# Applying the RMSNorm of the first token pair at the evictions, and moving weight fold and memory keys behind the first tiles

## The chip, the cores and the metric

One core of a Trainium2 chip runs the whole program. The metric is the device time of one execution in microseconds; three runs are shown, with their median.

## The reference

One layer of a streaming encoder on `x` (2048 tokens x 1024), f32:

```python
hn = rms_norm(x, norm_g)
proj = hn @ pool_w_in                       # 1024 -> u (768) | mq (256) | gate (1024)
u, mq, gate = split(proj)
# four groups of 192 columns: causal window means (2, 4, 8, 16) minus u, times w_group, times pool_scale
tok = multi_scale_pool(u, pool_w_group, pool_scale)
mem_k, mem_v = split(rms_norm(mem, mem_norm_g) @ w_mem_kv)   # 256 memory rows, 4 heads of 64
mem_o = softmax(mq @ mem_k.T / 8) @ mem_v
h = x + (concat(tok, mem_o) * silu(gate)) @ w_out
out = rms_norm(h, final_norm_g)
```

`rms_norm(x, g)` is `x * rsqrt(mean(x*x) + 1e-6) * g`, so a token's factor is one number that multiplies its whole projection.

## The kernel before, in words

Tokens are worked on transposed (channels on partitions) in four blocks of 512, two blocks making a pair. Every f32 product is three f32r products: each operand is split into a rounded high part and the rest (`_split`, L42 to L46), and `_mm3` (L49 to L53) adds high x high, high x low and low x high. A tile of weights is 128 output columns: 8 slices of 128 channels, 24 matmuls of 512 columns for each block. The first pair takes its tiles straight (`tile_in`, L425), 16 of them in the order of `TILES`: `q` are memory queries, `g` gates, `z` pooled columns. The second pair takes tiles two by two with seven products in place of eight (`group`, L388); its seven forms are prepared while the first pair runs (`stage_forms`, L238, four steps).

The pooled weights are folded first: `fold` (L280) multiplies the pooled part of `pool_w_in` by `w_group` in eight steps `k`, writes each into `w_z` in DRAM, and the `z` tiles load it from there. `wus` holds the eight loads `w_uT`, `wga` and `wgb` the group weights.

`first_block` (L211) makes a block ready: `squares` (L205) sums each row of `x` on ACT, `rstd_of` (L179) takes the power on POOL, `bcast_cols` (L191) broadcasts the four columns by matmuls with the identity, then for each of 8 slices DVE multiplies by gain and factor, ACT casts the high part and DVE subtracts the low one. So nothing of a block can be multiplied before its rows have been summed. `memory` (L324) makes `khi`, `klo` and `vhl` from `mem`, and `Attention` (L515) computes scores, softmax and mix in steps. `row_stats` (L230) sums the rows of the second pair and sends their factors through DRAM (`rows`).

`between()` is called after each half tile of a block; `Steps` (L691) counts these calls and runs the functions hooked to a number, and attention steps. That gives the order of the program; a scheduler then moves instructions within it by buffers and readiness, except loads that `load` (L115) keeps in program order. Each engine and each DMA queue (SP, ACT, POOL) runs its list in order. Tiles come from pools: `raw` has four buffers for loaded weights, `ch` four pairs for split weights, `ps_mm` four product banks, `sgp` two, `up` two.

The results leave a bank by a `take` function: queries are cast and subtracted straight from the bank (L446), gates go through Silu on ACT (L457), pooled columns are copied by ACT (L507). In the second pair `rest` is a tile to be added on DVE first (L104).

```python
fold()
xa = first_block(0)
xcol.append(load_columns(1, (8, 9)))
loaded = load_memory()
TILES = [("q", 0, (0,)), ("q", 1, (0,)), ("g", 5, (0, 1)), ("q", 0, (1,)), ("q", 1, (1,))]
hooks = {8: [lambda: memory(loaded)], 16: [stats]}
```

Of the kernel before, what the change touches and what calls it, by code (L numbers as in the profile page):

```python
# [56 lines left out]
def trunk(ctx, tc, x, xT, mem, memT, norm_g, mem_norm_g, w_mem, w_out, w_in, w_uT, w_g, p_scale, final_g,  # L57
# [53 lines left out]
    for _ in range(7):  # L111
        nc.tensor.matmul(idle, lhsT=zeros[:, :P], rhs=zeros, start=True, stop=True)
# [7 lines left out]
    wga = raw_tile((P, 4, GD))  # L120
    wgb = st.tile([P, 2, GD], F32, name="s")
    wus = [t[:, :6 * P].rearrange("p (g d) -> p g d", g=6) for t in long_tiles() + [zz((P, D)) for _ in range(4)]]
    for g in range(0, 4, 2):
        load(out=wga[:, g:g + 2], in_=w_g[g:g + 2, 0:128, :].rearrange("g c e -> c g e"))
        load(out=wus[0][:, g:2 + 2 * g], in_=w_uT[0, :, g:2 + 2 * g])
    for l in range(2):
        load(out=wgb[64 * l:64 * l + 64], in_=w_g[l::2, 128:192, :].rearrange("g c e -> c g e"))
    for k in range(1, KT):
        load(out=wus[k], in_=w_uT[k])
# [23 lines left out]
    xrow = [load_rows_of(0, (8, 9), load)]  # L153
    xcol = [load_columns(0, (12, 13))]
    ahead = [load_tile(w_in[j], load) for j in range(2)]
    xrow.append(load_rows_of(1, (10, 11), load))
# [29 lines left out]
    def rows_sq(src, t, acc):  # L186

        sp.dma_start(out=t, in_=src)
        nc.scalar.activation(out=t, in_=t, func=AF.Square, accum_out=acc)
# [21 lines left out]
    def first_block(a):  # L211

        rb = sgp.tile([P, BT], F32, name="sg")
        bcast_cols(squares(xrow[a]), QT, rb)
        hl = [(slot(2 * a + 4 * kh), slot(2 * a + 4 * kh + 1)) for kh in range(2)]
        for k in range(KT):
            v = xcol[a][k // KH][:, k % KH, :]
# [12 lines left out]
    def row_stats(s):  # L230

        rows = dram.tile([2, QT, P], F32, name="rows")
        for a in range(2):
            r = load_rows_of(2 * s + a, (10 + 2 * a, 11 + 2 * a), sp.dma_start)
            sp.dma_start(out=rows[a].rearrange("t p -> p t"), in_=squares(r))
        return rows
# [43 lines left out]
    def fold():  # L280

        tails = [[pl.tile([P, 2, GD], F32R, name=n) for _ in range(2)] for pl, n in ((att, "pr"), (up, "u"))]
# [6 lines left out]
        for k in range(KT):  # L289
            zs = wus[k].rearrange("p g d -> p (g d)")  # L290
            ut = ch.tile([P, 2, 2, P], F32R, name=("wh", "wl")[k % 2])
            nc.scalar.copy(ut[:, 0], wus[k][:, 4:6, :])
            nc.gpsimd.tensor_tensor(out=ut[:, 1], in0=wus[k][:, 4:6, :], in1=ut[:, 0].bitcast(F32), op=ALU.subtract)
            pss = [ps_mm.tile([P, 2, GD], F32, name="mm") for _ in range(2)]
            for a, ps in enumerate(pss):
                for l in range(2):
                    nc.tensor.matmul(ps[:, l, :], lhsT=wus[k][:, 2 * a + l, :], rhs=wga[:, 2 * a + l, :], start=l == 0,
                                     stop=False)
                _mm3(nc, ps, ut[:, 0, a, :], ut[:, 1, a, :], tails[0][a], tails[1][a], False, True)
# [3 lines left out]
            nc.scalar.dma_start(out=w_z[:, :, k, :].rearrange("j p f -> p j f"), in_=wus[k])  # L303
# [11 lines left out]
    def load_memory():  # L315
        mts = [long("mq").rearrange("p (k n) -> p k n", k=4) for _ in range(2)]
        wrs = [long(n) for n in ("pth", "ptl")]
        for c in range(2):
            load(out=mts[c], in_=memT[c])
        for c in range(2):  # L320
            load(out=wrs[c].rearrange("p (k n) -> p k n", k=2), in_=w_mem[c])
        return mts, wrs

    def memory(loaded):  # L324
        mh, ml = ([zz((P, 4, NMEM), F32R) for _ in range(2)] for _ in range(2))
        ssm = small.tile([P, 2], F32, name="ssm", bufs=1)
        mts, wrs = loaded
# [9 lines left out]
        for c in range(4):  # L337
            if c > 1:
                wrs.append(long("mq"))
                sp.dma_start(out=wrs[c].rearrange("p (k n) -> p k n", k=2), in_=w_mem[c])  # L340
            wr = wrs[c].rearrange("p (k n) -> p k n", k=2)
# [10 lines left out]
        for t in range(2):  # L352
            rows_sq(mem[t * P:(t + 1) * P, :], long(("pth", "ptl")[t]), ssm[:, t:t + 1])
        rm = rstd_of(ssm, 2)
        rmb = up.tile([P, NMEM], F32, name="u")
# [32 lines left out]
    def group(X, pair, take, between):  # L388
# [26 lines left out]
        take(0, 0, product(2, 1), None)  # L415
# [5 lines left out]
        take(1, 1, p7, u4)  # L421
        take(0, 1, product(3, 5), u2)
        take(1, 0, product(4, 7), u2)

    def tile_in(xs, wr, take, between):  # L425

        ps = {a: ps_mm.tile([P, BT], F32, name="mm") for a in xs}
        for kh in range(2):
            hi, lo = chunk(wr[:, kh * KH:(kh + 1) * KH], "act", (P, KH, P))
# [5 lines left out]
        for a in xs:  # L435
            take(0, a, ps[a], None)

    def take_query(s, p0):
        def take(i, a, ps, rest):
            p = p0 + i  # L440
            src = ps
            if rest is not None:
                src = sgp.tile([P, BT], F32, name="sg")
                add(nc.vector, src, ps, rest)
# [6 lines left out]
    def take_gate(s, j):  # L451
        def take(i, a, ps, rest):
# [8 lines left out]
    def take_pool(s, j0):  # L461
# [39 lines left out]
        def take(i, a, ps, rest):  # L501
# [6 lines left out]
            else:  # L508
                add(nc.vector, v, ps, rest)
# [176 lines left out]
    fold()  # L686
    xa = first_block(0)
    xcol.append(load_columns(1, (8, 9)))
    loaded = load_memory()
# [15 lines left out]
    def tile_of(s, kind, j, xs, between):  # L705
        if kind == "q":
            wr = ahead.pop(0) if ahead else load_tile(w_in[j])
            tile_in(xs, wr, take_query(s, j), between)
        elif kind == "g":
            tile_in(xs, load_tile(w_in[2 + j]), take_gate(s, j), between)  # L710
        else:
            tile_in(xs, load_tile(w_z[j]), take_pool(s, j), between)

    state = {}
    X1 = {}

    def stats():
        sp.dma_start(out=ci, in_=cinv)
        state["rows"] = row_stats(1)

    def stage(k):
        if not X1:
# [105 lines left out]
```

## Time and profile before

| | |
|---|---|
| three runs, us | 663.74, 663.86, 664.25 (median 663.86) |
| the profiled execution's own time, us | 666.16 |
| its span, first to last instruction, us | 664.4 |
| granted TensorE clock, mean | 0.955 |
| busy: PE, weight loads, DVE, ACT, POOL | 606.2, 505.6, 405.7, 332.2, 147.9 us |
| moved by DMA | 125.47 MB, mean 189 GB/s |

PE is TensorE's matmuls, PEld its weight loads, DVE VectorE, ACT ScalarE, POOL GpSimd; SPq, ACTq and POOLq are the queues that issue DMAs. Clock 1.00 is 2.4 GHz and half of it 1.2. In a row of the trace `mm<-x,wh` says what an instruction writes and reads, and an idle time in brackets names who ended it. Shares over the span are means over stretches with different limits.

### The profile page before, as it was taken

The numbers are of one execution on the slowest core, as the hardware profiler recorded it, in microseconds if no ns is written. First come the engines' busy times: TensorE is split into PE (matmuls) and PEld (weight loads), VectorE is DVE, ScalarE is ACT, GpSimd is POOL, SyncE is SP. The second block draws the span as 40 slices with busy tenths as digits, with TensorE's granted clock in tenths as the row PEclk, the third lists the DMA queues.
The fourth block names the chain that finished last, engine by engine and source line by source line (L and its number), as shares of the span: only waits on it lengthen the run. The fifth ranks groups of instructions, "written<-read, shape, count | busy, mean of one in ns | idle before, by whom it ended". The sixth has DMA issues, their size and how long they took to land.

```text
span 664.4 us, 8391 instructions
## 1 busy us (share of the span) xinstructions
PE 606.2 (91%) x2827; PEld 505.6 (76%) x2827; DVE 405.7 (61%) x677; ACT 332.2 (50%) x690; POOL 147.9 (22%) x157
## 2 busy tenths in 40 slices
PE   7649587799999999999999899998999999999993
PEld 6638476687787888888888688886788888888882
DVE  2055843748888446478578976799883436715126
ACT  3356741733766765474685398853652423214112
POOL 2101030115435113100006700163200001206016
PEclk7879689799998999999999899999999999999997
DMA  8999535675666541765441443337895136960006
GB/s 302 377 353 416 220 111 99 193 247 199 205 199 220 191 144 63 246 204 177 166 151 40 148 145 120 128 120 238 292 408 211 47 126 206 336 250 1 1 0 254
DMA packets 56123, 125.47 MB, mean 189 GB/s; under 512 B 7824, under 2 KB 17424, under 8 KB 56080
## 3 DMA queue, kind: packets, MB, share of 16 engines
q1 hardware_dynamic: 41056, 104.47, 46.5%
q10 hardware_dynamic: 13744, 16.27, 6.9%
q0 software_dynamic: 1280, 4.20, 1.7%
q8 instruction: 22, 0.36, 0.3%
q14 instruction: 21, 0.17, 0.1%
HBM read 87.68 MB, written 36.70 MB: 187 GB/s over the span
## 4 chain that ended last, share of the span: by engine, by line
PE 56%; DVE 15%; DMA 12%; ACT 8%; issue 5%; POOL 2%; SPq 1%; ACTq 0%; POOLq 0%; DVEq 0%
PE mm L52 13%; PE mm L51 13%; PE mm L53 13%; DVE wl L46 3%; DMA raw<-in_xT 2%; PE pt L52 2%; PE sc L53 2%; PE pt L53 2%; PE sc L52 2%; PE sc L51 2%; PE pt L51 2%; DMA w_z<-mq 2%; DVE zz L497 2%; DMA rows<-rstd 2%; DVE raw L101 1%
## 5 line engine op out<-in xcount | busy, mean ns | idle before, releaser
L51 PE MATMUL mm<-x,wh 128*128 128x512 f32 x480 | 192.2, 401 | 12.8 <-ACT wh L38 7.2
L52 PE MATMUL mm<-x,wh 128*128 128x512 f32 x480 | 190.6, 398 | 4.6 <-DVE x L46 4.6
L53 PE MATMUL mm<-x,wl 128*128 128x512 f32 x480 | 188.1, 396 | 0.0
L46 DVE TENSOR_TENSOR wl<-raw,wh 128x512 fp32r<-128x512 f32 x108 | 85.9, 802 | 87.5 <-ACT wh L38 87.5
L38 ACT CAST wh<-raw 128x512 fp32r<-128x512 f32 x108 | 66.2, 618 | 117.7 <-PE pt L53 80.0
L482 POOL TENSOR_TENSOR zz<-zz 128x527 f32<-128x527 f32 (+6 forms) x64 | 82.4, 1296 | 163.9 <-ACT zz L507 101.3
L51 PEld LDWEIGHTS mm<-x,wh 128*128 128x128 f32 x480 | 92.0, 192 | 32.3 <-ACT wh L38 7.9
L52 PEld LDWEIGHTS mm<-x,wh 128*128 128x128 f32 x480 | 92.0, 192 | 22.8 <-DVE x L46 4.8
L53 PEld LDWEIGHTS mm<-x,wl 128*128 128x128 f32 x480 | 91.8, 191 | 18.5 <-DVE wl L46 0.3
L52 PE MATMUL mm<-wl,x 128*128 128x512 f32 x128 | 49.8, 389 | 0.0
L51 PE MATMUL mm<-wh,x 128*128 128x512 f32 x128 | 49.7, 389 | 0.0
L53 PE MATMUL mm<-wh,x 128*128 128x512 f32 x128 | 49.7, 389 | 0.0
L634 POOL TENSOR_TENSOR rstdo<-sso,half 128x1 f32<-128x1 f32 x16 | 14.7, 918 | 129.6 <-DVE sso L676 129.6
L547 ACT ACTIVATE pr<-sc,nm 128x256 f32<-128x256 f32 x64 | 29.8, 471 | 22.9 <-DVE nm L543 22.2
L552 ACT ACTIVATE pr<-pr,rc 128x256 f32<-128x256 f32 x64 | 29.1, 503 | 8.7 <-DVE rc L550 8.4
L38 ACT CAST x<-raw 128x512 fp32r<-128x512 f32 x28 | 16.7, 620 | 24.4 <-DVE raw L249 10.4
L543 DVE TENSOR_REDUCE nm<-sc 128x2 f32<-128x512 f32 x32 | 21.8, 683 | 10.7 <-PE sc L541 10.5
L52 PEld LDWEIGHTS mm<-wl,x 128*128 128x128 f32 x128 | 24.0, 188 | 5.0
L51 PEld LDWEIGHTS mm<-wh,x 128*128 128x128 f32 x128 | 24.0, 188 | 5.0
L53 PEld LDWEIGHTS mm<-wh,x 128*128 128x128 f32 x128 | 24.0, 188 | 4.9
L249 DVE SCALAR_TENSOR_TENSOR raw<-raw,gx,s 128x512 f32<-128x512 f32 x16 | 13.0, 851 | 23.9 <-DMA raw<-in_xT 23.9
L38 ACT CAST x<-zz 128x512 fp32r<-128x512 f32 x32 | 18.2, 617 | 14.5 <-DMA zz<-br_d 6.3
(191 smaller groups left out, 1065.0 us busy)
## 6 DMA issues: line engine op xcount, KB each, us to landing
raw<-in_w_in SPq DMA_DIRECT2D x22, 512.0 KB, 5.1
x<-in_x SPq DMA_DIRECT2D x16, 512.0 KB, 8.0
g_d<-sg ACTq DMA_DIRECT2D x32, 256.0 KB, 3.3
raw<-in_w_out SPq DMA_DIRECT2D x16, 512.0 KB, 4.4
raw<-w_z SPq DMA_DIRECT2D x12, 512.0 KB, 4.1
sg<-g_d SPq DMA_DIRECT2D x24, 256.0 KB, 3.5
br_d<-zz SPq DMA_DIRECT2D x12, 512.0 KB, 3.7
x<-in_xT SPq DMA_DIRECT2D x8, 512.0 KB, 9.3
```

Source lines behind the costliest of these rows:

```text
L38: return nc.scalar.copy(hi, src)
L46: return e.tensor_tensor(out=lo, in0=src, in1=hi.bitcast(F32), op=ALU.subtract)
L51: nc.tensor.matmul(ps, lhsT=ahi, rhs=bhi, start=start, stop=False, **kw)
L52: nc.tensor.matmul(ps, lhsT=ahi, rhs=blo, start=False, stop=False, **kw)
L53: nc.tensor.matmul(ps, lhsT=alo, rhs=bhi, start=False, stop=stop, **kw)
L249: nc.vector.scalar_tensor_tensor(out=rt[:, a, :], in0=rt[:, a, :], scalar=gx[:, kk:kk + 1], in1=rb[a], op0=ALU.mult, op1=ALU.mult)
L482: nc.gpsimd.tensor_tensor(out=cur[rows, c0:c1], in0=prev[rows, c0:c1], in1=prev[rows, c0 - step:c1 - step], op=ALU.add)
L497: nc.vector.scalar_tensor_tensor(out=v, in0=v, scalar=psc[:, j:j + 1], in1=gates[a], op0=ALU.mult, op1=ALU.mult)
L543: nc.vector.tensor_reduce(out=nm, in_=ps, axis=AX.X, op=ALU.max, negate=True)
L547: nc.scalar.activation(out=pr[:, h, :], in_=ps[:, h, :], func=AF.Exp, bias=nm[:, h:h + 1], accum_out=su[:, h:h + 1])
L552: nc.scalar.mul(pr[:, h, :], pr[:, h, :], rc[:, h:h + 1])
L634: nc.gpsimd.tensor_tensor(out=ro, in0=sso[:, 1, t:t + 1], in1=half[:, :1], op=ALU.pow)
```

## The change

Four things. The first pair's blocks are no longer multiplied by the tokens' factors: `first_block` now casts gain x column on ACT (`nc.scalar.mul`) and takes the low part in one DVE operation, and `first_norm` makes the broadcast factors later, in `norms[a]`; `tile_in` multiplies a bank by them at its eviction, on DVE, with `take`'s new `op`. Evictions that come before the factors wait in `unscaled`. The loads begin with the first query tile's halves and the columns, then come the rows. The two query weight tiles are split once for both blocks (`qws`), and both query tiles of both blocks come first. `fold` and the memory's loads run after tile g5 (step 12), `memory` at 17, the row statistics at 18 and 21, attention from 20; the fold's weights go through the four `raw` buffers, and its stores from ACT's queue to SP's. The copies of `khi` and `klo` go from ACT's queue to POOL's. Ten idle matmuls, not seven, stand at the start.

```diff
-    for _ in range(7):
+    for _ in range(10):
...
+    wq0, first = load_q(0)
+    xcol = [[slot(n, dt=F32) for n in (8, 9)]]
+    for kh in range(2):
+        first[kh]()
+        for k in range(0, KH, 2):
+            load(out=xcol[0][kh][:, k:k + 2, :], in_=xT[0, :, kh * KH + k:kh * KH + k + 2, :])
+    ahead = [wq0, load_tile(w_in[1], load)]
+    xcol.append(load_columns(1, (10, 11)))
+    xrow = [load_rows_of(0, (12, 13), load)]
+    ahead.append(load_tile(w_in[7], load))
+    xrow.append(load_rows_of(1, (8, 9), load))
...
     def bcast_cols(r, n, dst):
-        ps = ps_mm.tile([P, BT], F32, name="mm")
+        ps = (ps_t if n == QT else ps_mm).tile([P, BT], F32, name="pt" if n == QT else "mm")
+        rb = sgp.tile([P, BT], F32, name="sg")[:, :n * P].rearrange("p (t f) -> p t f", t=n)
+        nc.vector.tensor_copy(rb, r[:, :n].unsqueeze(2).broadcast_to([P, n, P]))
         for t in range(n):
-            rb = small.tile([P, P], F32, name="rb", bufs=1)
-            nc.vector.tensor_copy(rb, r[:, t:t + 1].broadcast_to([P, P]))
-            nc.tensor.matmul(ps[:, t * P:(t + 1) * P], lhsT=rb, rhs=ident, start=True, stop=True)
+            nc.tensor.matmul(ps[:, t * P:(t + 1) * P], lhsT=rb[:, t, :], rhs=ident, start=True, stop=True)
...
     def first_block(a):
-        rb = sgp.tile([P, BT], F32, name="sg")
-        bcast_cols(squares(xrow[a]), QT, rb)
...
-            nc.vector.scalar_tensor_tensor(out=v, in0=v, scalar=gx[:, k:k + 1], in1=rb, op0=ALU.mult, op1=ALU.mult)
-            _split(nc, hl[k // KH][0][:, k % KH, :], hl[k // KH][1][:, k % KH, :], v, "act")
+            nc.scalar.mul(hi, v, gx[:, k:k + 1])
+            nc.vector.scalar_tensor_tensor(out=lo, in0=v, scalar=gx[:, k:k + 1], in1=hi.bitcast(F32), op0=ALU.mult,
+                                           op1=ALU.subtract)
...
+    def first_norm(a):
+        norms[a] = up.tile([P, BT], F32, name="u")
+        bcast_cols(squares(xrow[a]), QT, norms[a])
...
         for k in range(KT):
+            wu = raw_tile((P, 6, P))
+            sp.dma_start(out=wu, in_=w_uT[k])
...
-            nc.scalar.dma_start(out=w_z[:, :, k, :].rearrange("j p f -> p j f"), in_=wus[k])
+            sp.dma_start(out=w_z[:, :, k, :].rearrange("j p f -> p j f"), in_=wu)
...
-                nc.scalar.dma_start(out=khi[o, p, h, :].bitcast(F32), in_=khi[r, p, h, :].bitcast(F32))
-                nc.scalar.dma_start(out=klo[o, p, h, :].bitcast(F32), in_=klo[r, p, h, :].bitcast(F32))
+                nc.gpsimd.dma_start(out=khi[o, p, h, :].bitcast(F32), in_=khi[r, p, h, :].bitcast(F32))
+                nc.gpsimd.dma_start(out=klo[o, p, h, :].bitcast(F32), in_=klo[r, p, h, :].bitcast(F32))
...
         for a in xs:
-            take(0, a, ps[a], None)
+            def scaled(a=a):
+                take(0, a, ps[a], ALU.mult, norms[a])
+            if a in norms:
+                scaled()
+            else:
+                unscaled[a].append(scaled)
...
-                add(nc.vector, sg, ps, rest)
+                nc.vector.tensor_tensor(out=sg, in0=ps, in1=rest, op=op)
...
+    TILES = [("q", 0, (0,)), ("q", 1, (0,)), ("q", 0, (1,)), ("q", 1, (1,))]
...
+    hooks = {7: [lambda: norm(0)], 10: [lambda: norm(1)], 12: [fold, lambda: loaded.extend(load_memory())],
+             17: [lambda: memory(loaded)], 18: [lambda: stats(0)], 21: [lambda: stats(1)]}
     for k in range(KH):
-        hooks[24 + 7 * k] = [lambda k=k: stage(k)]
-    steps = Steps(0, 18, 2.5, hooks)
-    xs = {0: xa}
+        hooks[25 + 7 * k] = [lambda k=k: stage(k)]
+    steps = Steps(0, 20, 2.5, hooks)
+    xs = {0: first_block(0)}
```

How the instructions stand now, at three places. `DMAHW` names a lane of the DMA queues that must have finished, an engine's name a wait for that engine; `x_n` are slots for columns, rows and split blocks.

TensorE behind the idle matmuls, before: the fold (L297 and `_mm3`, its group weights in `raw`) is the first work.

```order
L112 MATMUL pt<-u 128x512
L297 MATMUL mm<-raw,mq 128x192 [waits DMAHW2_49,DMAHW1_49]
L297 MATMUL mm<-raw,mq 128x192
L297 MATMUL mm<-raw,mq 128x192 [waits DMAHW6_49,DMAHW4_49]
L297 MATMUL mm<-raw,mq 128x192
L51 MATMUL mm<-pr,wh 128x384 [waits DVE_49,Activation_49]
```

The same engine now, where the fold (L307, its group weights in `pth`) begins: six tile-blocks stand ahead of it, and the second block's broadcast (L201) among the last matmuls of g5.

```order
L201 MATMUL pt<-ident,sg 128x128 [waits DVE_49,PE_49]
L201 MATMUL pt<-ident,sg 128x128 x3
L52 MATMUL mm<-x_265,wh 128x512
L53 MATMUL mm<-x_264,wl 128x512
L51 MATMUL mm<-x_264,wh 128x512
L52 MATMUL mm<-x_265,wh 128x512
L53 MATMUL mm<-x_264,wl 128x512
L307 MATMUL mm<-pth,raw 128x192 [waits DMAHW5_49,DMAHW1_49,DVE_49]
L307 MATMUL mm<-pth,raw 128x192
L51 MATMUL mm<-pr,wh 128x384 [waits Activation_49]
```

The fold moved from the head of the list to behind six tile-blocks.

Queue SP now, in the middle of the fold: the stores of steps one to four (L313), loads of the attention's query tile `mq` (L557, L558), and the weights of steps five to eight (L299).

```order
L313 DMA w_z<-raw 128x6x128 [waits DMAHW2_49,Activation_49]
L557 DMA mq<-q_d_174 64x512 [waits DMAHW3_49,DVE_49]
L558 DMA mq<-q_d_174 64x512 [waits DMAHW4_49]
L557 DMA mq<-q_d_174 64x512 [waits DMAHW5_49]
L558 DMA mq<-q_d_174 64x512 [waits DMAHW6_49]
L557 DMA mq<-q_d_174 64x512 [waits DMAHW7_49,DVE_49]
L299 DMA raw<-in_w_uT 128x768 [waits DMAHW0_49,PE_49,Pool_49]
L558 DMA mq<-q_d_174 64x512 [waits DMAHW1_49]
L557 DMA mq<-q_d_174 64x512 [waits DMAHW2_49]
L299 DMA raw<-in_w_uT 128x768 [waits DMAHW3_49,PE_49,Pool_49]
```

Before, all eight loads of `w_uT` stood among the first thirteen of this queue and the stores in ACT's; now loads that wait for DVE stand ahead of the fifth.

DVE before, behind the memory part: the low halves of weights (L46), keys and values, then the second pair's columns (L249).

```order
L360 TENSOR_TENSOR pr<-sc,u 128x256 [waits PE_49] x2
L46 TENSOR_TENSOR wl<-raw,wh 128x512 [waits Activation_49]
L46 TENSOR_TENSOR klo<-pr,khi 64x256 [waits Activation_49] x4
L368 TENSOR_SCALAR pr<-pt,rstd 128x256 [waits DVE_49]
L368 TENSOR_SCALAR pr<-pt,rstd 128x256 [waits DVE_49,PE_49]
L249 SCALAR_TENSOR_TENSOR raw<-raw,gx,s 128x512 [waits DMAHW4_49]
L249 SCALAR_TENSOR_TENSOR raw<-raw,gx,s 128x512 [waits DMAHW5_49]
```

DVE now, within the memory part, whose weights `x_631` and `x_634` give the low halves `wl`:

```order
L478 TENSOR_TENSOR sg<-mm,u 128x512 [waits DMAHW7_49,PE_49]
L46 TENSOR_TENSOR wl<-x_631,wh 128x512 [waits DMAHW2_49,DVE_49,Pool_49]
L199 COPY sg<-rstd 128x256 [waits DMAHW4_49,Activation_49]
L256 SCALAR_TENSOR_TENSOR raw<-raw,gx,s 128x512 [waits DMAHW5_49,DMAHW2_49,DMAHW1_49]
L46 TENSOR_TENSOR wl<-x_631,wh 128x512 [waits Pool_49]
L256 SCALAR_TENSOR_TENSOR raw<-raw,gx,s 128x512 [waits DMAHW7_49]
L46 TENSOR_TENSOR wl<-x_634,wh 128x512 [waits Pool_49] x2
```

The second pair's columns (L256, L249 before) moved ahead of five of the memory's eight low halves, and an eviction (L478) stands in this list that was ACT's.

## Rows read from the trace of the kernel before

**Rows 1.** Windows: stretch, length, busy us (count) of engines, PE clock, DMA share, GB/s
```profile
0.00:49.40 49.40, 30.82 (x128) 26.16 (x128) 13.14 (x32) 19.88 (x43) 8.17 (x16) 0.79 0.99 343
49.40:122.10 72.70, 55.23 (x259) 46.53 (x260) 37.51 (x76) 35.82 (x70) 8.72 (x13) 0.85 0.66 212
160.00:210.00 50.00, 44.96 (x217) 36.93 (x216) 42.25 (x66) 32.58 (x72) 21.05 (x23) 0.97 0.61 197
210.00:290.00 80.00, 80.00 (x406) 68.00 (x405) 44.44 (x80) 46.96 (x102) 15.70 (x20) 1.00 0.49 162
```

**Rows 2.** Timeline of PE, last row of ACT: start us, us, instruction, count, idle before
```profile
1.30 3.17 PE L112 MATMUL pt<-u 128*128 128x512 bf16 x7 [1.30 <-POOL u L108]
...
19.66 0.81 PE L297 MATMUL mm<-raw,zz 128*128 128x192 f32 x4
...
22.00 0.81 PE L297 MATMUL mm<-raw,zz 128*128 128x192 f32 x4
...
30.44 1.65 PE L297 MATMUL mm<-raw,zz 128*128 128x192 f32 x4 [5.93 <-ACT zz L302]
...
107.10 0.39 PE L51 MATMUL mm<-x,wh 128*128 128x512 f32 x1
...
111.63 0.39 PE L53 MATMUL mm<-x,wl 128*128 128x512 f32 x1
...
120.46 0.55 PE L541 MATMUL sc<-klo,mq 128*128 128x256 f32 x1 [6.01 <-DMA klo<-klo]
...
299.40 0.57 ACT L412 COPY u<-mm 128x512 f32<-128x512 f32 x1
```

**Rows 3.** Waits up to 140 us: who, for whom, us in total, times, longest
```profile
ACT zz L302 <- DMA w_z<-mq: 7.5, 1, 7.5
...
ACT vhl L38 <- DMA klo<-klo: 15.6, 1, 15.6
...
DVE raw L249 <- DMA raw<-in_xT: 14.8, 2, 14.5
```

**Rows 4.** DMA rates up to 140 us, 40 slices of 3.5 us
```profile
GB/s 104 236 364 417 422 390 408 369 337 383 395 266 355 357 407 409 420 421 420 391 334 11 150 150 110 117 94 207 1 5 9 138 267 244 165 123 253 187 248 386
```

**Rows 5.** Timelines of DVE and ACT; groups (count, busy us, mean ns, idle before)
```profile
42.17 5.39 DVE L218 SCALAR_TENSOR_TENSOR x<-x,gx,sg 128x512 f32<-128x512 f32 x8
...
39.72 0.86 ACT L302 COPY zz<-mm 128x384 f32<-128x384 f32 x2 [2.18 <-DMA ci<-in_cinv]
...
62.18 1.71 ACT L333 ACTIVATE zz<-mq,gm 128x256 fp32r<-128x256 f32 x4
...
63.91 1.28 ACT L457 ACT_TABLE_LOAD   x1
...
L208 ACT ACTIVATE x<-x 128x1024 f32<-128x1024 f32 x16 | 16.8, 1050 | 0.0
...
L104 DVE TENSOR_TENSOR sg<-mm,u 128x512 f32<-128x512 f32 x15 | 10.3, 686 | 3.7 <-DMA g_d<-sg 1.9 <-PE mm L53 1.7
...
L101 DVE TENSOR_TENSOR raw<-raw 128x512 f32<-128x512 f32 x13 | 13.8, 1083 | 0.1
...
L457 ACT ACTIVATE sg<-sg 128x512 f32<-128x512 f32 x12 | 7.6, 631 | 0.4 <-DVE sg L104 0.3
```

**Rows 6.** DMA issues over the span: queue, count, KB each, median us to landing
```profile
mq<-in_w_mem SPq DMA_DIRECT2D x2, 512.0 KB, 3.2
...
w_z<-mq ACTq DMA_DIRECT2D x2, 384.0 KB, 12.9
...
g_d<-sg ACTq DMA_DIRECT2D x32, 256.0 KB, 3.3
...
rows<-rstd SPq DMA_DIRECT2D x2, 2.0 KB, 10.1
...
s<-rows SPq DMA_DIRECT2D x8, 256.0 KB, 4.5
...
xs_d<-raw POOLq DMA_DIRECT2D x12, 256.0 KB, 2.9
```

More of the change, by code (lines that the diff above doesn't have):

```diff
@@ L151, in load_tile, with load_q @@
         return wr
[L153 to L156, printed above, removed]
+    def load_q(j):
+        wr = raw_tile((P, KT, P))
+        return wr, [lambda h=h: load(out=wr[:, h * KH:(h + 1) * KH], in_=w_in[j, :, h * KH:(h + 1) * KH]) for h in range(2)]
+    wq0, first = load_q(0)
[9 more added lines that the diff above has]
+    xrow.append(load_rows_of(1, (8, 9), load))
+    wga = att.tile([P, D], F32, name="pth", bufs=1)[:, :4 * GD].rearrange("p (g e) -> p g e", g=4)
+    wgb = st.tile([P, 2, GD], F32, name="s")
+    load(out=wga, in_=w_g[:, 0:128, :].rearrange("g c e -> c g e"))
+    for l in range(2):
+        load(out=wgb[64 * l:64 * l + 64], in_=w_g[l::2, 128:192, :].rearrange("g c e -> c g e"))
+    mts = [att.tile([P, 4, NMEM], F32, name="mq") for _ in range(2)]
     def load_pair(w1, w2, how=sp.dma_start):
@@ L228, in combine, with row_stats @@
         sub(g, t4, b21, t2)
[L230 to L236, printed above, removed]
+    def row_stats(s, a, rows):
+        r = load_rows_of(2 * s + a, (10 + 2 * a, 11 + 2 * a), sp.dma_start)
+        sp.dma_start(out=rows[a].rearrange("t p -> p t"), in_=squares(r))
     def stage_forms(s, k, rows, X):
@@ L280, in fold @@
     def fold():
-        tails = [[pl.tile([P, 2, GD], F32R, name=n) for _ in range(2)] for pl, n in ((att, "pr"), (up, "u"))]
+        low = att.tile([P, D], F32R, name="ptl", bufs=1)[:, :4 * GD].rearrange("p (a l e) -> p a l e", a=2, l=2)
+        tails = [[att.tile([P, 2, GD], F32R, name="pr") for _ in range(2)], [low[:, a] for a in range(2)]]
         for t in tails[0] + tails[1]:
@@ L315, in load_memory @@
     def load_memory():
-        mts = [long("mq").rearrange("p (k n) -> p k n", k=4) for _ in range(2)]
-        wrs = [long(n) for n in ("pth", "ptl")]
         for c in range(2):
[L319 to L322, printed above, removed]
+            sp.dma_start(out=mts[c], in_=memT[c])
+        wrs = []
+        for n in (8, 9):
+            t = slot(n, (P, 2, 2, 2 * NMEM), F32)
+            for i in range(2):
+                sp.dma_start(out=t[:, i], in_=w_mem[len(wrs)])
+                wrs.append(t[:, i])
+        rows = [long(n) for n in ("pth", "ptl")]
+        for t in range(2):
+            sp.dma_start(out=rows[t], in_=mem[t * P:(t + 1) * P, :])
+        return wrs, rows
     def memory(loaded):
@@ L352, in memory @@
         for t in range(2):
-            rows_sq(mem[t * P:(t + 1) * P, :], long(("pth", "ptl")[t]), ssm[:, t:t + 1])
+            nc.scalar.activation(out=rows[t], in_=rows[t], func=AF.Square, accum_out=ssm[:, t:t + 1])
         rm = rstd_of(ssm, 2)
-        rmb = up.tile([P, NMEM], F32, name="u")
+        rmb = sgp.tile([P, BT], F32, name="sg")[:, :NMEM]
         bcast_cols(rm, 2, rmb)
@@ L414, in group @@
         add(nc.vector, u2, p6, u2)
-        take(0, 0, product(2, 1), None)
+        take(0, 0, product(2, 1), None, None)
         sub(g, a12, a12, s2)
@@ L443, in take @@
                 src = sgp.tile([P, BT], F32, name="sg")
-                add(nc.vector, src, ps, rest)
+                nc.vector.tensor_tensor(out=src, in0=ps, in1=rest, op=op)
             q = zz((P, 2, BT), F32R)
@@ L508, in take @@
             else:
-                add(nc.vector, v, ps, rest)
+                nc.vector.tensor_tensor(out=v, in0=ps, in1=rest, op=op)
             left[i] -= 1
@@ L706, in tile_of, with stats @@
         if kind == "q":
-            wr = ahead.pop(0) if ahead else load_tile(w_in[j])
-            tile_in(xs, wr, take_query(s, j), between)
+            tile_in(xs, ahead[j], qws[j], take_query(s, j), between)
         elif kind == "g":
-            tile_in(xs, load_tile(w_in[2 + j]), take_gate(s, j), between)
+            tile_in(xs, ahead[2] if j == 5 else load_tile(w_in[2 + j]), [], take_gate(s, j), between)
         else:
-            tile_in(xs, load_tile(w_z[j]), take_pool(s, j), between)
+            tile_in(xs, load_tile(w_z[j]), [], take_pool(s, j), between)
+    qws = [[], []]
     state = {}
     X1 = {}
-    def stats():
-        sp.dma_start(out=ci, in_=cinv)
-        state["rows"] = row_stats(1)
+    def stats(a):
+        if not a:
+            sp.dma_start(out=ci, in_=cinv)
+            state["rows"] = dram.tile([2, QT, P], F32, name="rows")
+        row_stats(1, a, state["rows"])
     def stage(k):
```

65 lines of the change are left out of this document (26 added, 39 removed).

## The prediction

> **What bounds the kernel now.** I read first the busy time of the engines in four stretches [rows 1]; the columns to compare are TensorE (PE), VectorE (DVE), the granted clock and the DMA share. From 210 us on TensorE is busy without a break at clock 1.00. In the first 49 us it is busy 30.8 of 49.4 us at clock 0.79, in the next 73 us 55.2 of 72.7 at 0.85. So nearly all that is left to win lies ahead of 122 us, and I ask how much work was done there.
>
> Three prices of TensorE's work at the higher clock, from its timeline [rows 2]. Between the two rows at 107.10 and 111.63 lie 20 steps of 512 columns: 0.2265 us each, so 24 of them (one weight tile against one token block, a tile-block below) are 5.44 us. One step of the fold takes from 19.66 to 22.00, 2.34 us; eight are 18.7. The memory part is 96 matmuls of half the columns: 10.9. At the lower clock everything takes double: the seven idle matmuls took 3.17 us, 0.45 each.
>
> At 120.46, where the first scores go on after waiting for `klo` [rows 2], before has done the fold, the memory part and six tile-blocks: 18.7 + 10.9 + 32.6 = 62.2 us of work. It has lost 58.3 us, and 299.40, where the second pair's first product is copied out, is later by as much.
>
> The waits tell why [rows 3]. ACT stood 7.5 us in front of a copy of the fold because a `w_z` store stood ahead of it in its queue, and 15.6 us behind the copies of `khi` and `klo`; DVE stood 14.8 us for the second pair's columns. And the DMA engines are full (share 0.99) for 49 us, since the fold's weights and the rows come ahead of the columns.
>
> **The change, part by part.** The common point is the start of tile g3: ten tile-blocks, fold and memory done, no scores yet. Before would be there at 120.5 + 4 x 5.44 = 142.3. The change has 84.0 us of work up to it (62.2 + 21.8); I add its idle time in order.
>
> *Start, +7.2.* The columns of both blocks and two weight tiles are 5.24 MB. The rates of the first slices, 3.5 us each, sum to 3.92 MB at 14 us and 5.40 at 17.5 [rows 4], so the last columns land at 17.1. DVE needs 0.67 us for each of 16 new subtractions (the like operation, eight in 5.39) and about as much for four weight halves: 13.5 us from 5.6, so it keeps pace [rows 5]. The ten idle matmuls end at 5.8 and TensorE follows the columns: the first tile-block ends near 12.7, the other three 16.3 later, at 29.0. The norm no longer stands ahead; it would have come first at 22.4 (7.34 MB) plus a square of 1.05, the power and the broadcast.
>
> *The norm at the evictions, +2.8.* All four product banks are full at 29.0. Broadcast 0.5, its copy 0.7, the first multiplication 0.69 [rows 5], and only then is a bank free: 1.9 us. For the second block 0.9, since its matmuls fall inside g5. The fold starts at 42.7.
>
> *Fold, first four steps, +5.6.* Work 9.4. But ACT's order puts between its copies of the results (0.43 each) a table load (1.28), two Silus (0.63), a cast and four squares of the second pair's rows (1.05) [rows 5]: from 46.2 some 10.2 us up to the fourth step's cast, then the low half on POOL and its matmuls, 57.7.
>
> *The gap in the fold, +9.3.* Queue SP holds loads of `mq` ahead of the weights of steps five to eight, and they wait until the memory's 16 scaling operations have read the two tiles of that name. ACT does them after the fourth copy: eight at 0.43 from 58.6 [rows 5], DVE done 62.5, five issues at about 0.5 until 63.5, and a load of some 3.5 us (a load of 512 KB in a calm queue: 3.2) [rows 6]: 67.0. Its low bound is 7, with no issue queued.
>
> *Clock, +3.0.* After a gap of 5.93 us TensorE came back at the lower clock: the row at 30.44 took 1.65 us for what took 0.81 at 19.66 [rows 2]. I take a step and a quarter at double time, 3.0 us, as an estimate. So the other four steps end at 79.4.
>
> *Tile g4, +1.7.* Its weights take the buffer of step five, so they wait for that step's store (issued 72.4). Stores of 384 KB took 12.9 us in the full queue; a store of 256 KB in a calm one 3.3 [rows 6]. The stream of loads, 17.4 MB up to step four's weights, is spent by about 47 us at these rates, so I take 4. Load 4, cast 0.6: 81.1, and g4 ends at 92.0. Tile z5 needs the last store (82.2 + 4) and a load: 91.7, hidden by 0.3 us. If that cover goes, z5 is late by whatever the stores cost more.
>
> *Memory and z5, +6.8.* DVE now has the first column scaling of the second pair (L256) in front of the memory's fourth low half. It waits for the rows' statistics: POOL has them at 87, SP stores them behind z5's load at 88, the store takes 10.1 and the broadcast load 4.5 [rows 6]: 103. TensorE has 7 us of work from 92, stands from 99 to 104.3 and pays 1.5 for the clock. Then 7.3 + 1.5 and the rest of z5: 120.4.
>
> Sum of idle 36.4 against 58.3: **21.9 us earlier** at the common point.
>
> *The heads' keys.* The eight copies of `khi` and `klo` go from ACT's queue to POOL's, where a landing took 2.9 [rows 6]; the first scores now stand among g3's matmuls. I cost them at nothing: cover is z5's last quarter of 7.3 us; without it 6.0, what the row at 120.46 waited [rows 2]. The trace shows that a queue is more than issue time: ACT's 7.5 and 15.6 us were waits for queued DMAs to finish [rows 3]. The Trainium skill, page "DMA: Bandwidth & Descriptors", section "Issuing engines are not separate DMA queues", says that starting DMAs on several engines only saves the sequencer's time; by it this move saves about the issues alone, the 6.0 us come back, and the time would be 650. The rows above speak against reading it so, as it is the queue's owner that stood still.
>
> *After the common point, -2.4.* Eleven tiles, 22 blocks, are now evicted on DVE with a multiplication of 0.69 instead of on ACT: 15.1 us. DVE is busy 42.3 of 50 us from 160 to 210, and 44.4 of 80 after [rows 1]. In the dense 50 us about seven evictions (4.8 us) fit in what is free, barely. I take half, 2.4; bounds 0 and 15.1, nearest the low end because each eviction has a tile's length to wait in.
>
> Net 21.9 - 2.4 = 19.5 us. The profiled run has a span of 664.4 and a time of 666.2; the median shown, 663.9, is 2.3 lower. Against the median: **644.4 us**.
>
> **The rivals.**
> *The gaps close further.* If DVE's wait for the statistics ends before the fourth low half (-6.8) and ACT does its squares in gaps (-5.6): 632. For it: DMA is calmer then than at 97 us in before. Against: the store of the statistics is 10.1 us whatever stands around it.
> *Stores stay dear.* At 12.9 us for both stores in series, g4 and z5 each come about 8.8 later: 662. For it: the one price that the trace shows for such a store. Against: the stream is over by then.
> *DVE becomes the bound of the first pair: slower.* Evictions of 1.083 us, as subtractions beside POOL's window sums took [rows 5], 22 times, all on TensorE's path, in place of the 2.4 taken: 644.4 - 2.4 + 23.8 = 665.8. It decides once DVE's share from the common point to the pair's end reaches one. Against: the same form with one input in PSUM took 0.686 at the mean [rows 5], and 36 of 80 us were free after 210.
> *The bytes decide anyway: no change.* The same loads are needed by the first scores and the DMA share is 0.99 for 49 us. If they ended last, order would not matter: 664. Against: the share is 0.66 from 49 to 122 us [rows 1], so the stream ends before the work does.
>
> **How the numbers follow.** Forecast (638 to 652) 0.58; gaps closing further (628 to 638) 0.17; dear stores (652 to 662) 0.14; no change 0.05; DVE as the bound 0.06. A measurement of this kernel can tell 0.2%, 1.3 us, from nothing. Faster by more: 0.58 + 0.17 + 0.14 = 0.89; same 0.05; slower 0.06. The range takes the forecast, most of the gaps and half of the dear stores: 631 to 657.
>
> **What would show it.** Right: TensorE's first product near 6 us and g5 started near 31; ACT idle little from 46 to 58; one gap of TensorE of 7 to 10 us inside the fold that a load of `w_uT` ends; DVE waiting at L256 near 100 us while TensorE stands; the second pair's first copy near 280 instead of 299.4. Wrong: stores of `w_z` still above 10 us; TensorE's waits after 125 us ended by DVE, with DVE near full until the pair's end; or a wait of scores for `klo` again.

## The result, and the profile after

The changed kernel takes **655.3 us** (median of four runs, 654.59 to 657.26) against 664.1 of the kernel before on the same chip: ratio 0.9866, 95% interval 0.9836 to 0.9897. That is 8.8 us faster. The forecast was 644.4, 19.5 us faster: the sign was right, the size less than half. The profiled execution has a span of 655.5 us and a time of 657.26; it is the slowest of the four.

Windows of the changed kernel, with the stretches and columns of [rows 1]:

```profile
0.00:49.40 49.40, 44.07 (x191) 33.30 (x191) 28.07 (x52) 31.69 (x55) 5.46 (x12) 1.00 0.99 375
49.40:122.10 72.70, 50.82 (x253) 45.45 (x252) 15.89 (x33) 25.07 (x52) 11.60 (x17) 0.81 0.69 201
160.00:210.00 50.00, 43.90 (x207) 35.43 (x206) 45.05 (x67) 28.63 (x58) 20.91 (x25) 0.97 0.66 231
210.00:290.00 80.00, 80.00 (x399) 67.49 (x399) 56.70 (x101) 52.62 (x111) 12.50 (x15) 1.00 0.50 165
```

The first 49 us went as meant: TensorE is busy 44.1 us instead of 30.8, at clock 1.00 instead of 0.79. The next 73 us got worse: 50.8 us of 72.7 at clock 0.81, where before had 55.2 at 0.85. DVE, with its new multiplications, is busy 45.1 of 50 us in the dense stretch (42.3 before), and TensorE is busy 1 us less there; but the stretch holds other work than before, some 10 us further on.

Where that second stretch is lost shows in the timeline of the changed kernel's TensorE (last row ACT, the second pair's first copy):

```profile
7.03 0.49 PE L51 MATMUL mm<-x,wh 128*128 128x512 f32 x1 [1.28 <-ACT x L220]
...
30.84 1.05 PE L201 MATMUL pt<-ident,sg 128*128 128x128 f32 x8
33.49 0.47 PE L51 MATMUL mm<-x,wh 128*128 128x512 f32 x1 [1.60 <-DVE sg L467]
...
45.93 0.92 PE L307 MATMUL mm<-pth,raw 128*128 128x192 f32 x4 [0.36 <-DVE sg L467]
...
69.50 2.90 PE L307 MATMUL mm<-pth,raw 128*128 128x192 f32 x8 [9.57 <-DMA raw<-in_w_uT]
83.74 0.50 PE L51 MATMUL mm<-x,wh 128*128 128x512 f32 x1 [2.39 <-ACT wh L38]
...
86.38 0.63 PE L53 MATMUL mm<-x,wl 128*128 128x512 f32 x1
...
96.39 0.39 PE L51 MATMUL mm<-x,wh 128*128 128x512 f32 x1
...
109.25 0.77 PE L201 MATMUL mm<-ident,sg 128*128 128x128 f32 x2 [5.71 <-DVE sg L199]
...
112.61 0.80 PE L53 MATMUL sc<-zz,wl 128*128 128x256 f32 x2 [0.89 <-DVE wl L46]
...
129.94 0.28 PE L563 MATMUL sc<-khi,mq 128*128 128x256 f32 x1
...
288.79 0.58 ACT L424 COPY u<-mm 128x512 f32<-128x512 f32 x1
```

Two stops stand out: 9.57 us inside the fold, ended by a load, and 5.71 us in the memory part, ended by DVE's L199. The wait in front of L199, in DVE's timeline, and the transfers issued from 92 to 110 us (KB each, median us to landing) tell about the second:

```profile
96.61 0.68 DVE L478 TENSOR_TENSOR sg<-mm,u 128x512 f32<-128x512 f32 x1
97.21 0.69 DVE L46 TENSOR_TENSOR wl<-x,wh 128x512 fp32r<-128x512 f32 x1
108.81 0.29 DVE L199 COPY sg<-rstd 128x256 f32<-128x256 f32 x1 [10.91 <-DMA g_d<-sg]
111.21 0.75 DVE L256 SCALAR_TENSOR_TENSOR raw<-raw,gx,s 128x512 f32<-128x512 f32 x1 [2.10 <-DMA s<-rows]
```
```profile
DMA packets 2089, 2.61 MB, mean 145 GB/s; under 512 B 1156, under 2 KB 1156, under 8 KB 2088
...
g_d<-sg ACTq DMA_DIRECT2D x2, 256.0 KB, 12.2
s<-rows SPq DMA_DIRECT2D x2, 256.0 KB, 3.3
rows<-rstd SPq DMA_DIRECT2D x2, 2.0 KB, 15.7
```

The second pair's statistics, 2 KB for each block in pieces of four bytes, took 15.7 us instead of the 10.1 of [rows 6]. And beside them two gates' stores took 12.2 us, where [rows 6] has 3.3. The memory's broadcast (L199) needs a buffer of `sg` that one of these stores held.

### The profile page after: what moved, and what is told of

It is laid out like the page before. It is cut to its first block, busy times and chain, and to the rows that moved or that the text cites. A ratio compares the mean times of both kernels' runs of the same rounds, so it can differ in the third digit from the quotient of the medians.

```text
span 655.5 us, 8373 instructions
## 1 busy us (share of the span) xinstructions
PE 604.3 (92%) x2830; PEld 500.2 (76%) x2830; DVE 410.7 (63%) x682; ACT 327.1 (50%) x674; POOL 150.5 (23%) x165
## 4 chain that ended last, share of the span: by engine, by line
PE 55%; DVE 15%; DMA 14%; ACT 7%; issue 5%; POOL 2%; SPq 1%; ACTq 0%; POOLq 0%; DVEq 0%
PE mm L51 13%; PE mm L52 13%; PE mm L53 13%; DVE wl L46 3%; DMA q_d<-zz 2%; DMA rows<-rstd 2%; PE sc L53 2%; PE pt L53 2%; PE pt L52 2%; PE sc L52 2%; PE sc L51 2%; PE pt L51 2%; DMA raw<-in_xT 2%; DVE raw L256 2%; DVE zz L520 1%
## 5 line engine op out<-in xcount | busy, mean ns | idle before, releaser
L46 DVE TENSOR_TENSOR wl<-raw,wh 128x512 fp32r<-128x512 f32 x104 | 83.8, 809 | 103.3 <-ACT wh L38 103.0
L38 ACT CAST wh<-raw 128x512 fp32r<-128x512 f32 x104 | 63.8, 617 | 118.7 <-PE pt L53 79.8
L657 POOL TENSOR_TENSOR rstdo<-sso,half 128x1 f32<-128x1 f32 x16 | 14.7, 918 | 129.6 <-DVE sso L699 129.6
L478 DVE TENSOR_TENSOR sg<-mm,u 128x512 f32<-128x512 f32 x28 | 19.1, 687 | 9.5 <-PE mm L53 6.9
L53 PE MATMUL sc<-wh,x 128*128 128x512 f32 x64 | 24.9, 389 | 0.0
```

Source lines behind the costliest of these rows:

```text
L38: return nc.scalar.copy(hi, src)
L46: return e.tensor_tensor(out=lo, in0=src, in1=hi.bitcast(F32), op=ALU.subtract)
L53: nc.tensor.matmul(ps, lhsT=alo, rhs=bhi, start=False, stop=stop, **kw)
L478: nc.vector.tensor_tensor(out=sg, in0=ps, in1=rest, op=op)
L657: nc.gpsimd.tensor_tensor(out=ro, in0=sso[:, 1, t:t + 1], in1=half[:, :1], op=ALU.pow)
```

## The experiments

All ratios are to the kernel before on the same chip, with 95% intervals. First the changed kernel again, as a yardstick.

> The changed kernel unaltered, on the chip of the three runs beside it, as their yardstick. Expected 654 to 657 us, with the same stall of TensorE near 103 to 109 us (5.7 us in front of the memory's broadcast) and the same gap of 9 to 10 us inside the fold.

Measured 654.6 us, 0.9876 (0.9856 to 0.9897). The stops again: 9.40 us in the fold, 3.39 and 2.21 in the memory part; first score at 128.48, second pair's first copy at 288.03.

**Statistics ahead of the memory part.**

```diff
-    17: [lambda: memory(loaded)], 18: [lambda: stats(0)], 21: [lambda: stats(1)]}
+    17: [lambda: stats(0), lambda: stats(1), lambda: memory(loaded)]}
```

> Edit: both calls of the second pair's row statistics stand ahead of the memory part in the program (DVE takes their variances before the memory's scaling; SP stores them among the fold's stores near 54 to 62 us instead of at 92). Theory A (the late statistics are what the memory stage lost: column scaling on DVE in front of the memory's low halves): the wait of that scaling for the broadcast rows goes, the stall of 5.7 us shrinks to under 2, the time falls by 5 to 7 us, to about 649. Rival B (the buffer of the memory's own broadcast, held by a gate's store, is the bound by itself): the stall stays near 5, gain under 1.5 us. Rival C (two stores in four-byte pieces among the fold's stores hold them up): the fold's gap grows from 9.6 to 13 or more, no gain or up to 3 us slower.

Measured 655.2 us, 0.989 (0.9868 to 0.9911): no gain. The stall in the memory part went, as theory A said (no wait of TensorE there), but the gap in the fold doubled, as rival C said. TensorE's timeline and the transfers issued from 52 to 68 us:

```profile
81.40 2.90 PE L307 MATMUL mm<-pth,raw 128*128 128x192 f32 x8 [20.73 <-DMA raw<-in_w_uT]
```
```profile
w_z<-raw SPq DMA_DIRECT2D x4, 384.0 KB, 14.7
mq<-q_d SPq DMA_DIRECT2D x1, 128.0 KB, 11.6
rows<-rstd SPq DMA_DIRECT2D x2, 2.0 KB, 15.6
```

The fold's stores landed after 14.7 us (6.2 in the changed kernel). The loss moved with the store.

**Statistics in rows of 512 bytes.**

```diff
-        sp.dma_start(out=rows[a].rearrange("t p -> p t"), in_=squares(r))
+        ps = ps_t.tile([P, BT], F32, name="pt")
+        nc.tensor.matmul(ps[:QT, :P], lhsT=squares(r), rhs=ident, start=True, stop=True)
+        rt = small.tile([P, P], F32, name="rt", bufs=1)
+        nc.scalar.copy(rt[:QT], ps[:QT, :P])
+        sp.dma_start(out=rows[a], in_=rt[:QT])
```

> Edit: the row statistics are turned by one matmul with the identity and stored as four rows of 512 bytes instead of 512 pieces of four bytes. Theory A (the small pieces make the store slow, 15.7 us, and hold up the gate's store behind it in the same DMA engines, which keeps the buffer of the memory's broadcast): the store lands in about 3 us, the gate's store issued at the same time in about 4 instead of 10, the stall of TensorE of 5.7 us goes to under 1, time 649 to 650. Rival B (the stores wait for other traffic, their pieces do not matter): landing above 8 us, stall unchanged, time within 1 us of the changed kernel.

Measured 645.2 us, 0.9735 (0.9712 to 0.9758), 9.4 us faster than the yardstick. The window from 92 to 109 us in this kernel and the gates' stores in it:

```profile
92.00:109.00 17.00, 17.00 (x114) 15.60 (x113) 8.17 (x14) 2.51 (x4) 5.24 (x10) 1.00 0.36 140
```
```profile
DMA packets 997, 2.37 MB, mean 132 GB/s; under 512 B 101, under 2 KB 101, under 8 KB 996
...
g_d<-sg ACTq DMA_DIRECT2D x2, 256.0 KB, 2.7
```

TensorE is busy for the whole of it, the gates' stores land in 2.7 us, and the first score is at 119.62, 8.9 earlier. That is theory A, with 4 us more than it gave. But the statistics now went out at 120 us, not 92, so the place had changed too. A control keeps the matmul, the copy and the order, and stores the same numbers from a column in four-byte pieces:

```diff
-        nc.tensor.matmul(ps[:QT, :P], lhsT=squares(r), rhs=ident, start=True, stop=True)
-        nc.scalar.copy(rt[:QT], ps[:QT, :P])
-        sp.dma_start(out=rows[a], in_=rt[:QT])
+        nc.tensor.matmul(ps[:, :QT], lhsT=ident, rhs=squares(r), start=True, stop=True)
+        nc.scalar.copy(rt[:, :QT], ps[:, :QT])
+        sp.dma_start(out=rows[a].rearrange("t p -> p t"), in_=rt[:, :QT])
```

> Control for store_rows: the same matmul, copy and place in the program (order of DVE as there), but the result of the matmul stays as a column and is stored in four-byte pieces. In store_rows the statistics were stored at 120 to 124 us, behind the memory part, in place of 92, so two things had changed. Theory A (place decides: out of the memory's way, the small pieces hurt nobody whom TensorE waits for): within 2 us of store_rows (645), no stall between 95 and 112 us, landing still 10 us or more, seen only in DVE's column scaling. Theory B (pieces decide wherever they stand): 650 to 655, TensorE or DVE waits 5 us or more behind these stores after 120 us.

Measured 660.7 us, 0.9989 (0.9973 to 1.0005): worse than the changed kernel, and by ratio 2.6% behind `store_rows`, and 5 us above the range of theory B. The stores landed in 9.4 us at the median, the first with almost nothing beside it (1 GB/s from 119 to 131 us). DVE stood 9.66 us for the first and 7.93 for the second, and TensorE then waited for ACT:

```profile
rows<-rt SPq DMA_DIRECT2D x2, 2.0 KB, 9.4
```
```profile
133.15 1.41 DVE L260 SCALAR_TENSOR_TENSOR raw<-raw,gx,s 128x512 f32<-128x512 f32 x2 [9.66 <-DMA s<-rows]
```
```profile
PE pt L590 <- ACT pr L579: 13.1, 4, 5.1
```

What SP's load of the statistics waited for the two stores gives the price of the layout itself, with the same order on both sides; first `same_path` (110 to 145 us), then `store_rows` (112 to 130):

```profile
SPq L253 <- DMA rows<-rt: 18.1, 2, 10.3
```
```profile
SPq L253 <- DMA rows<-rt: 1.7, 2, 0.9
```

The pieces decide, wherever they stand; the place decides who pays for them. Two layouts and two places make four cells; the last one is early and in rows (`stats_first` and `store_rows` together):

> Edit: stats_first and store_rows together, so the statistics are stored among the fold's stores, as in stats_first, but as rows of 512 bytes. Theory B (pieces decide): the gap inside the fold returns from 20.7 us to 10, landing of the statistics and of the fold's stores falls to 4 to 6, no stall in the memory part, time 644 to 647. Theory A (place decides): the gap stays above 15 us and the time at 652 to 656, as in stats_first.

Measured 646.2 us, 0.9771 (0.9747 to 0.9795). Gap and transfers of 52 to 68 us:

```profile
70.47 2.90 PE L311 MATMUL mm<-pth,raw 128*128 128x192 f32 x8 [9.81 <-DMA raw<-in_w_uT]
```
```profile
w_z<-raw SPq DMA_DIRECT2D x4, 384.0 KB, 5.7
```

Theory B again: at the same place in the program the fold's stores land in 5.7 us instead of 14.7, and the gap is back at 9.81. One caution: of the two statistics' stores only the first (58.83 us) went out among the fold's first four here, the second at 70.18; in `stats_first` both did.

**A buffer of its own for the memory's broadcast.** L199 copies into tiles of `small` and `rmb` lies in `pr`, so no gate's store is in the way.

```diff
...
-        rmb = sgp.tile([P, BT], F32, name="sg")[:, :NMEM]
+        rmb = att.tile([P, NMEM], F32, name="pr")
```

> Edit: the memory's broadcast has buffers of its own, so it no longer waits for a gate's store to free one; the statistics and their store stay as they are, and DVE still has the second pair's column scaling in front of the memory's fourth low half. Theory of the prediction (that scaling, which waits for the statistics to come back from memory, holds the low halves): TensorE still stands 3 to 7 us between 103 and 113 us, now ended by a low half on DVE, time within 2 us of the changed kernel's 654.6. Rival (the buffer held by the gate's store is the bound): the stall goes, time 648 to 650.

Measured 655.0 us, 0.9887 (0.986 to 0.9914): no gain. DVE's and TensorE's timelines:

```profile
108.33 0.75 DVE L262 SCALAR_TENSOR_TENSOR raw<-raw,gx,s 128x512 f32<-128x512 f32 x1 [11.44 <-DMA s<-rows]
```
```profile
110.76 0.79 PE L53 MATMUL sc<-zz,wl 128*128 128x256 f32 x2 [6.50 <-DVE wl L46]
```

With the buffer free the column scaling that the prediction named (L256, here L262) holds the low halves as long. Two waits stood side by side, both on the slow store; the one that ends last hides the other.

**SP's queue in another order.** The fold's last four weight loads are issued behind the first four stores, the scores' first query loads after the fold.

```diff
+            if k < 4:
+                weights(k + 4, load)
...
+                    how = load if self.s == 0 and i < QT + 1 else sp.dma_start
```

> Edit: SP's queue issues the fold's last four weight loads directly behind the first four stores, and the first eight loads of the scores' queries after all of the fold. Theory (the gap inside the fold is the query loads that stand in front and wait for the memory's scaling): the gap of 9.6 us falls to 4 to 5 (what a store of 5 us and a load of 5 us leave), the fold ends about 5 us earlier, and the time falls by 3 to 5 us. Rival (the buffers come free no earlier because the first four stores take as long): gap still above 8 us, gain under 1 us. A third outcome: the fold ends earlier but the memory stage still waits for the statistics and their store, which do not depend on it: gain under 2 us although the gap shrinks.

Measured 647.4 us, 0.977 (0.9748 to 0.9793), 7.2 faster than the yardstick. The gap:

```profile
66.06 2.90 PE L314 MATMUL mm<-pth,raw 128*128 128x192 f32 x8 [5.56 <-DMA raw<-in_w_uT]
```

So the query loads did hold the weights back, for 4 us of the gap. The first score comes 5.5 us earlier (122.93), the second pair 9.5 (278.53); where the rest came from was not separated.

**Both together, and all three.**

> Edit: store_rows and sp_order together. If the two losses are separate, in series on TensorE's path, their gains add: 654.6 - 9.4 - 7.2 = 638. If both run into the same later wait, the sum is less: 642 to 645. First scores expected near 116 us (128.5 in the changed kernel, 119.6 and 122.9 in the two alone).

Measured 642.8 us, 0.9721 (0.9699 to 0.9743), hardly more than the rows alone by ratio, so the two gains do not add. The first score came at 124.02, not near 116 as expected. The statistics went out at 116 to 120 us, and DVE stood 6.13 us for them until 123. With the statistics early as well (`stats_first`, `store_rows` and `sp_order`):

> Edit: rows_first and sp_order together (statistics early and stored as rows of 512 bytes; SP's queue loads the fold's weights ahead of the scores' queries). If the order on SP is worth the 7 us that it brought alone: 639. If what counts after 130 us is another limit (DVE or the forms of the second pair), as rows_sp suggests, where the two gains of 9.4 and 7.2 gave 11.9 together: 641 to 643.

Measured **640.5 us**, 0.9639 (0.9616 to 0.9662), 3.6% below before, the best version here, and between the two expectations. No wait for `rows` is left, and TensorE is busy 161.9 of the 165 us from 130 to 295 (158.6 in the changed kernel).

**The multiplications on DVE.** Gates and pooled columns go through ACT without the factors.

```diff
-            if rest is not None:
+            if rest is not None and op != ALU.mult:
...
-            if rest is None:
+            if rest is None or op == ALU.mult:
```

> Edit on the changed kernel: the gates and pooled columns of the first pair leave their banks through ACT again, without the tokens' factors (so their norm is left out of the computation; the queries keep it). It prices the multiplications on DVE. Theory (the term of 2.4 us after the common point, and 1.6 to 2.4 us ahead of the first tiles): first pair ends 2 to 4 us earlier, time 650 to 653. Rival (DVE is the bound of the first pair from 150 to 200 us, where it is busy 9 of 10 us or more): 8 us or more faster, 646 or less. Third: DVE was hidden there altogether, and ACT takes as long: within 1 us.

Measured 654.7 us, 0.986 (0.9838 to 0.9882): the third outcome.

> Edit: the same on store_rows (gates and pooled columns through ACT without the factors, norm left out there). Without the stall of the memory stage the dense stretch of DVE comes earlier. Theory as in act_evict: 1 to 4 us faster than store_rows' 645. Rival (with the stall gone DVE is the next bound): 8 us or more, 637 or less.

Measured 644.6 us, 0.9707 (0.9685 to 0.9728). Against their partners that is 0.2% and 0.3% by ratio, with overlapping intervals (in us: 0.1 slower and 0.7 faster). So the multiplications cost 0 to 2 us by these figures and at most some 4 by the intervals; the rival's 8 us are out.

**The keys' copies.** Back on ACT's queue (`nc.gpsimd.dma_start` to `nc.scalar.dma_start`, two lines):

> Edit on the changed kernel: the eight copies of khi and klo go back to ACT's queue. Theory of the prediction (costed at nothing on POOL; on ACT the wait of 6.0 us for klo comes back, since the copies stand among ACT's work behind casts and queued DMAs): up to 6 us slower, 657 to 661. Rival (a landing takes about 3 us on either queue once the DMA engines are calm, and the first scores have cover): within 1.5 us of the changed kernel's 654.6.

Measured 663.3 us, 0.9991 (0.9973 to 1.0008): 8.7 us slower than the yardstick (7.6 by ratio), and 2 us past the upper end expected. Landing and waits, the copies' rows for 100 to 160 us and TensorE's waits from 130 to 295 us:

```profile
khi<-khi ACTq DMA_DIRECT2D x4, 64.0 KB, 3.5
klo<-klo ACTq DMA_DIRECT2D x4, 64.0 KB, 3.4
```
```profile
PE sc L563 <- ACT pr L570: 7.7, 3, 4.3
PE pt L586 <- ACT pr L575: 1.9, 3, 0.9
```

The copies land as soon as on POOL's queue (3.4 and 3.1 us in the changed kernel), and the scores wait for no copy. But ACT stood 4.2 us behind them before the casts of `vhl`, and TensorE's waits for the softmax on ACT rose from 3.0 us (2.6 and 0.4) to 9.6. The scheduler also reordered much of ACT and DVE here, so how much is the queue and how much the order is open.

**Two parts on the kernel before.**

> Edit on the kernel before: its row statistics, too, are turned by a matmul and stored as rows of 512 bytes. Theory (the changed kernel uncovered this store: in before nothing on TensorE's path waited for it or for a transfer beside it, since the second pair's columns came last, 14.5 us of waiting on DVE at 120): within 2 us of before. Rival (the store cost before as much as the changed kernel): 6 to 10 us faster, so that the change itself, with the store taken away on both sides, brings no more than the 9 us that were measured.

Measured 658.6 us, 0.9952 (0.9933 to 0.9971), 3 us faster, between the two theories. The 6.0 us for `klo` [rows 2] are gone, and ACT's 15.6 us behind the copies [rows 3] became

```profile
ACT vhl L38 <- DMA khi<-khi: 5.6, 1, 5.6
```

In before the first copy of `khi` was issued at 107.38, though the casts began at 102.13; here at 102.34, right behind its cast. So before, too, the statistics' store (issued at 96.04, landing 10.1) seems to have held back the copies behind it. A control like `same_path` was not tried there, and what ties a store in SP's queue to copies in ACT's is open.

> Edit on the kernel before: only the eight copies of khi and klo go from ACT's queue to POOL's. Theory (the 6.0 us that the first scores waited for klo, and ACT's 15.6 us behind the copies, were waits of the queue's owner, and a landing on POOL's queue takes 3 us): 3 to 8 us faster. Rival (the queues share the DMA engines and the copies land no sooner; only their issue time is saved): within 1.5 us of before.

Measured 660.5 us, 0.9979 (0.9961 to 0.9996): 1.4 us, within the rival's bound, but not for the rival's reason. The trace agrees with the theory: with the pieces still in flight (issued at 94.58, landing 8.6) the first copy left at 100.80, 0.7 us behind the first cast instead of 5.2, and neither ACT's 15.6 us nor the scores' 6.0 are there. DVE still stood 10.9 us in front of the second pair's columns, and later TensorE stood for the softmax on ACT:

```profile
PE pt L563 <- ACT pr L552: 7.6, 1, 7.6
```

The scheduler also put the first score at 128.50 instead of 114.10. By these two runs the copies' delay in before needed both, ACT's queue and the store. Alone, the move to POOL's queue takes away the waits and brings little time.

## Why the prediction was wrong in size

Step by step, with the start of each stage as predicted and as the rows above show it (an end is the next start less the wait in front of it):

| start of | predicted | changed kernel | later than predicted, added here |
|---|---|---|---|
| norm of block 0 | 29.0 | 30.84 | 1.8 |
| fold | 42.7 | 45.93 | 1.4 |
| fold's step five | 67.0 | 69.50 | -0.7 |
| tile g4 | 81.1 | 83.74 | 0.1 |
| tile z5 | 92.0 | 96.39 | 1.8 |
| common point (first score) | 120.4 | 129.94 | 5.1 |

**The step that failed is "Memory and z5, +6.8".** Memory and z5 are 21.8 us of work and took 33.55, so the term measures 11.8 (9.1 in `a_again`). Two parts of it were too small. TensorE stood 6.6 us in its two stops, where 5.3 had been forecast; and behind the first stop it ran at the lower clock (0.50, so 1.2 GHz) from 109.25 to 118.50, an estimated 4.2 us lost (half of the 8.36 busy), where 1.5 had been charged:

```profile
109.25:118.50 9.25, 8.36 (x37) 8.07 (x38) 5.40 (x10) 0.62 (x1) 1.56 (x3) 0.50 0.28 79
```

The cause of the stop was right in part: L256 does wait for the statistics in front of the memory's low halves, and with the buffer freed it alone makes the stop (`own_rb`). But the price was taken from [rows 6] as 10.1 us, as if it were paid by the waiting instruction only. What the store costs its neighbours was not in the sum at all. With both blocks' statistics stored at 92 us and gates' stores issued into them, it became 15.7 and the gates' 12.2; and the wait that came first in the trace was L199's for such a gate's store, which the prediction did not have. With the pieces out of this stage no stop is left and the term is 1.4 (`store_rows`: 23.15 us from z5's start at 96.47 to the first score), and the time is 645.2, near the forecast's figure; that agreement is partly chance, since the steps ahead of the memory part were 4.4 us too early together. The term is as small in `same_path` (1.2), where the pieces go out late and TensorE's 13.1 us of waits lie behind the common point.

The rival that the gaps close further said "the store of the statistics is 10.1 us whatever stands around it". That sentence was wrong twice: it went from 9.4 in calm to 15.7 with its surroundings, and its size is a choice of the layout. The hint was in the trace of before: the store was issued at 96.0, and the keys' copies that took ACT's 15.6 us and the scores' 6.0 left from 107 on; I read these as two facts about two queues.

**The other terms.** *Start*: right in kind (first product 7.03, clock 1.00), 1.8 too early. *Norm at the evictions*: 1.4 short. *Fold, first half*: within 1 us. *Gap, 9.3*: 9.57, cause as written (`sp_order`). *Dear stores*, a rival at 0.14: no, `w_z` landed in 5.6 us over the first 300 us. *Tile g4*: its start was right, but it took 12.65 us instead of 10.9, because TensorE ran at the lower clock from 84.3 to 87.7, just behind its 2.39 us wait (rows of 0.63 us); the prediction charged that only after the longer stops. With the 2.7 us of the memory part (4.2 less 1.5), the lower clock makes an estimated 4.5 of the 9.5 us by which the common point was late. *After the common point, -2.4*: the lead fell from 12.4 us (142.3 less 129.9) to 10.6 (299.40 less 288.79), so 1.8 went: the size was right so far. At the end of the two profiled executions it is 8.9 (664.4 less 655.5); but from the second pair's first copy to the end `a_again` took 364.8 us, before 365.0 and this execution 366.7, so the last 1.7 is not the kernel's each time. Whether the multiplications are the cause of the 1.8 stays open, since without them the time changes by 0 to 2 us (`act_evict`, `rows_act`). The slower rival, DVE as the bound, wanted 23.8 us and falls by the same two runs, although DVE is busy 45 of 50 us.

*The keys' copies at nothing*: on POOL's queue they cost nothing. The Trainium skill, page "DMA: Bandwidth & Descriptors", section "Issuing engines are not separate DMA queues", says that starting DMAs on several engines saves the sequencer's time only. The landings on the changed kernel agree (3.4 to 3.5 us on ACT's queue, 3.1 to 3.4 on POOL's). The waits do not: in `before_keys` the move took away ACT's 15.6 us and the scores' 6.0, as the prediction had read [rows 3], though the time fell by 1.4 only. With the copies back on ACT's queue (`keys_act`) the changed kernel was 8.7 us slower, some of it perhaps by the other order; no score waited for `klo` there either, so the 6.0 us that made the 650 did not come back.

In sum: mending the store on both sides leaves the change itself at 0.9735 / 0.9952 = 0.978, some 14 us, of the 19.5 forecast.

## What to carry to other kernels

A store in four-byte pieces is slow itself and is paid by its neighbours too: look for any transfer in the same 10 us whose landing is longer than its like elsewhere, and write small vectors as rows (a matmul with the identity turns them). If a long wait has two causes on one slow transfer, removing one shows nothing; test the transfer itself. Charge the lower clock for as long as a trace shows it, behind short stops too. And when a scheduler's order puts a load that waits in front of one that could go, the second one's queue position is worth a run.

## What the runs showed of the hardware

Two stores of 2 KB in pieces of four bytes took 9.4 us at the median, one after the other and the first with the DMA engines otherwise all but empty (1 GB/s, `same_path`); as four rows of 512 bytes the load behind them waited 0.9 us at most, not 10.3. Stores of 256 KB from another queue took 12.2 us beside them instead of 2.7 (changed kernel, `store_rows`), stores of 384 KB from the same queue 14.7 instead of 5.7 (`stats_first`, `rows_first`).

The Trainium skill, page "DMA: Bandwidth & Descriptors", section "Specifications", gives 512 bytes as the least transfer for full rate and says that smaller ones are read, modified and written. The trace agrees that the smaller ones are dear; that they hold up the larger beside them is what these runs add.
